# Seven half-sized products instead of eight for 40 gate-and-up pairs of a two-layer decoder

## The chip, the cores and the metric

The kernel runs on one core of a Trainium2 chip. The metric is the time of one execution on the device in microseconds (us); the kernel before takes 2120.57 us, the median of 3 runs (2119.62 to 2121.41). The core has a matrix engine (TensorE, PE in the rows; its weight loads are PEld), a vector engine (VectorE, DVE), an activation engine (ScalarE, ACT), GpSimd (POOL) and an engine that issues transfers (SyncE, SP).

## The reference

Two layers of a decoder, each a feed-forward block at half step, a token mixer and a second feed-forward block, all in float32 on 512 tokens of width 1024. What matters here is the feed-forward block:

```python
def swiglu(h, w_in, w_out):                  # h (512, 1024), w_in (1024, 2*2816), w_out (2816, 1024)
    gate, up = jnp.split(h @ w_in, 2, axis=-1)
    return (jax.nn.silu(gate) * up) @ w_out

for l in range(DEPTH):                       # DEPTH = 2
    ...                                      # mod: nine vectors from c for shifts, scales and gates
    h = modulate(rms_norm(x, norm_g[l, 0]), sh1, sc1)
    x = x + FFN_HALF * gt1[:, None, :] * swiglu(h, ffn1_in[l], ffn1_out[l])
    ...                                      # the token mixer
    h = modulate(rms_norm(x, norm_g[l, 2]), sh2, sc2)
    x = x + FFN_HALF * gt2[:, None, :] * swiglu(h, ffn2_in[l], ffn2_out[l])
return rms_norm(x, final_norm_g)
```

## The kernel before

Activations lie with channels on the 128 partitions: `hh` and `hl` hold the block's input `h` as eight chunks of 128 channels by 512 tokens. Every float32 operand of a large product is held as two parts, a high part (`whi`, `hh`, `gh`) in the matrix engine's rounded format and the rest (`wlo`, `hl`, `gl`), and a product is three matmuls, high by high, high weights by low tokens and low weights by high tokens (`mm3`, lines 414 to 420).

The 2816 hidden channels are worked in two halves of 11 *pairs*. A pair is one block of 128 gate channels and the block of 128 up channels that goes with it: two weight tiles of 128 x 1024 (eight chunks), each multiplied with all 512 tokens into a bank of PSUM, 2 x 8 x 3 = 48 matmuls of 512 columns. Then `swiglu` takes the SiLU on ACT, multiplies on DVE and splits the result into `gh` and `gl`. The first two pairs of a first half are worked together, in halves of 256 tokens, because the norm of the second half of the tokens is still being computed then. After a half's 11 pairs come its eight output blocks (each 33 matmuls).

Weights come through `Weights` (lines 138 to 187). `plan` lists them all in the order of use. `dma_to` loads one into a ring of three raw tiles (`wraw`, 512 KB each; a load of the ring waits until the tile it takes has been split), `split_to` makes `whi` on ACT and `wlo` on DVE (for the second pair of a first half, on GpSimd) in rings of four, and `use` keeps the split two tiles ahead of the products and the loads five ahead. A scheduler then sets the order on each engine: it takes the earliest work that its own model says is ready, so that queues can hold work of several pairs interleaved.

In layer 1 DVE also computes the modulation vectors beside the products (line 256, `adaw`); in layer 2 there are none left. Layer 2's first feed-forward block stands at about 1065 to 1430 us of the profile, its second at 1749 to 2108 us.

Of the kernel before, what the change touches and what calls it, by code (L numbers as in the profile page):

```python
# [139 lines left out]
class Weights:  # L140
# [5 lines left out]
        self.units, self.raw, self.hl = [], {}, {}  # L146
        self.nd = self.ns = 0

    def add(self, ap, width, pool=False):
        self.units.append((ap, width, pool))  # L150
        return len(self.units) - 1

    def dma_to(self, i):
        while self.nd < len(self.units) and self.nd <= i:
            ap, w, _ = self.units[self.nd]
            t = self.pool.tile([128, D], F32, name="wraw", tag="wraw", bufs=self.br)
            dst = t[:, :w] if len(ap.shape) == 2 else t[:, :w].rearrange("p (i n) -> p i n", n=ap.shape[2])
            self.nc.sync.dma_start(dst, ap)
            self.raw[self.nd] = t
            self.nd += 1  # L160

    def split_to(self, i):
        while self.ns < len(self.units) and self.ns <= i:
            j = self.ns
            self.dma_to(j)
            _, w, pool = self.units[j]
# [14 lines left out]
    def use(self, i):  # L181
        self.advance(i)
        return self.hl.pop(i)


class Build:
    def __init__(self, tc, a, out, dbg=None, layers=L, stop=None):
        self.tc, self.nc, self.a, self.out, self.dbg = tc, tc.nc, a, out, dbg or (lambda *k: None)
        self.layers, self.stop = layers, stop
        self.bgq = []  # L190
        self.nbank = 0
        self.sql = {}

    def bg(self, n=1):
# [233 lines left out]
    def plan(self):  # L428
        W, a = self.W, self.a
        self.u = {}  # L430
        for l in range(self.layers):
            for which in (0, 1, 2):
                if which != 1:
# [47 lines left out]
    def ffn(self, l, which):  # L481
        nc = self.nc
        w = which // 2
        gate = self.mod[l]
        gh = self.gh = self.fp.tile([128, FH, T], F32R, name="gh")
        gl = self.gl = self.fp.tile([128, FH, T], F32R, name="gl", tag="gl")
        for half in range(2):
            i = 0
            if l == 0 and which == 0 and half == 0:
# [2 lines left out]
                self.first_gl = self.last_gl  # L492
                i = FIRST
            while i < FH:
                group = [i, i + 1] if (half == 0 and i == 0) else [i]
                i += len(group)
                js = [(j, s) for j in group for s in range(2)]
# [38 lines left out]
                self.bg(self.bg_rate)  # L536
            if tail:
                self.halves(range(KC - tail, KC), out_mm, gate, 24 * which + 16)

    def swiglu(self, j, pg, pu):  # L540
        nc = self.nc
# [593 lines left out]
    def open_ffn(self, ada, first=False):  # L1135
        self.fp_cm = self.tc.tile_pool(name="ffn", bufs=1, side="right", reuse_waits="tile")
        fp = self.fp = self.fp_cm.__enter__()
        self.open_sq(fp)
        if ada:
            self.cact = fp.tile([128, D], F32, name="cact")  # L1140
            if first:
# [101 lines left out]
```

## Time and profile before

| | |
|---|---|
| median of 3 runs | 2120.57 us |
| the profiled execution's own time | 2122.84 us |
| its span in the profile | 2121.1 us |
| mean granted clock of the matrix engine | 0.996 of full |
| PE, DVE, ACT, POOL busy | 99%, 52%, 38%, 10% |
| layer 2, first feed-forward block (1064.8 to 1430) | 365.2 us; PE 363.5, DVE 132.4, ACT 111.8, POOL 15.6 busy |
| layer 2, second feed-forward block (1749 to 2108) | 359.0 us; PE 359.0, DVE 125.3, ACT 108.2, POOL 9.5 busy |

Busy times are unions: a matmul's record covers its latency, and matmuls of one stream overlap, so what one costs is the distance from one start to the next and not its duration. For DVE, ACT and POOL a duration is nearly the cost of the instruction; successive ones overlap by about 0.1 us.

### The profile page before, as it was taken

The numbers are of one execution on the slowest core, as the hardware profiler recorded it, in microseconds if no ns is written. First come the engines' busy times: TensorE is split into PE (matmuls) and PEld (weight loads), VectorE is DVE, ScalarE is ACT, GpSimd is POOL, SyncE is SP. The second block draws the span as 40 slices with busy tenths as digits, with TensorE's granted clock in tenths as the row PEclk, the third lists the DMA queues.
The fourth block names the chain that finished last, engine by engine and source line by source line (L and its number), as shares of the span: only waits on it lengthen the run. The fifth ranks groups of instructions, "written<-read, shape, count | busy, mean of one in ns | idle before, by whom it ended". The sixth has DMA issues, their size and how long they took to land.

```text
span 2121.1 us, 27803 instructions
## 1 busy us (share of the span) xinstructions
PE 2093.0 (99%) x10938; PEld 1743.2 (82%) x10938; DVE 1108.0 (52%) x1731; ACT 796.3 (38%) x1309; POOL 211.0 (10%) x196
## 2 busy tenths in 40 slices
PE   9999999999999999999999999999999999999998
PEld 7888888988965988888888888889788669888887
DVE  8894333637875799533353333335578754333332
ACT  4422323543665522222342222234527654222323
POOL 1000001312301200000110000012223020000002
PEclk9999999999999999999999999999999999999999
DMA  9894323423310699432333233235232112233322
GB/s 342 310 358 156 91 83 100 144 90 96 96 40 19 236 359 339 159 99 78 91 110 93 82 114 99 75 98 166 82 90 79 31 35 85 91 89 113 96 80 80
DMA packets 93829, 269.10 MB, mean 127 GB/s; under 512 B 10865, under 2 KB 21985, under 8 KB 93698
## 3 DMA queue, kind: packets, MB, share of 16 engines
q1 hardware_dynamic: 92018, 266.06, 38.7%
q8 instruction: 86, 1.41, 0.3%
q0 software_dynamic: 672, 0.58, 0.2%
q10 hardware_dynamic: 1008, 0.69, 0.1%
q14 instruction: 45, 0.37, 0.0%
HBM read 259.94 MB, written 2.10 MB: 124 GB/s over the span
## 4 chain that ended last, share of the span: by engine, by line
PE 96%; DVE 2%; ACT 1%; issue 1%; POOL 0%; DMA 0%; POOLq 0%; DVEq 0%; ACTq 0%
PE mm L418 26%; PE mm L419 26%; PE mm L420 26%; PE o L1062 2%; PE mm L579 1%; PE t L1052 1%; PE mm L578 1%; PE mm L580 1%; PE mm L1020 1%; PE f L419 1%; PE f L418 1%; PE f L420 1%; PE mm L1021 1%; DVE hl L349 0%; PE o L756 0%
## 5 line engine op out<-in xcount | busy, mean ns | idle before, releaser
L170 ACT ACTIVATE whi<-wraw 128x1024 fp32r<-128x1024 f32 (+3 forms) x374 | 361.1, 966 | 1054.8 <-PE mm L419 971.8
L419 PE MATMUL mm<-hl,whi 128*128 128x512 f32 (+1 forms) x1736 | 654.8, 378 | 3.1 <-DVE hl L349 3.1
L420 PE MATMUL mm<-hh,wlo 128*128 128x512 f32 (+1 forms) x1736 | 654.5, 378 | 0.0
L418 PE MATMUL mm<-hh,whi 128*128 128x512 f32 (+1 forms) x1736 | 649.3, 378 | 2.8 <-ACT hh L378 2.2
L171 DVE TENSOR_TENSOR wlo<-wraw,whi 128x1024 fp32r<-128x1024 f32 (+2 forms) x354 | 390.7, 1104 | 447.7 <-ACT whi L170 440.6
L419 PEld LDWEIGHTS mm<-hl,whi 128*128 128x128 f32 x1736 | 328.6, 189 | 62.4 <-DVE hl L349 3.7
L418 PEld LDWEIGHTS mm<-hh,whi 128*128 128x128 f32 x1736 | 326.5, 189 | 64.0 <-issue 3.1
L420 PEld LDWEIGHTS mm<-hh,wlo 128*128 128x128 f32 x1736 | 328.3, 189 | 60.5 <-issue 2.0
L419 PE MATMUL mm<-gl,whi 128*128 128x512 f32 (+1 forms) x792 | 290.2, 366 | 0.0
L420 PE MATMUL mm<-gh,wlo 128*128 128x512 f32 (+1 forms) x792 | 289.6, 366 | 0.0
L418 PE MATMUL mm<-gh,whi 128*128 128x512 f32 (+1 forms) x792 | 289.1, 365 | 0.0
L301 POOL TENSOR_TENSOR sqa<-sqa,sq 128x512 f32<-128x512 f32 (+1 forms) x44 | 51.3, 1165 | 1433.2 <-ACT sq L300 1125.8
L544 DVE TENSOR_TENSOR sg<-sg,mm 128x512 f32<-128x512 f32 x85 | 58.4, 687 | 227.5 <-PE mm L420 225.0
L256 DVE SCALAR_TENSOR_TENSOR adaw<-adaw,cact 128x1024 f32<-128x1024 f32 x144 | 171.7, 1217 | 6.6 <-ACT cact L1150 6.6
L419 PEld LDWEIGHTS mm<-gl,whi 128*128 128x128 f32 x792 | 149.4, 189 | 24.3
L420 PEld LDWEIGHTS mm<-gh,wlo 128*128 128x128 f32 x792 | 149.4, 189 | 24.0
L418 PEld LDWEIGHTS mm<-gh,whi 128*128 128x128 f32 x792 | 149.4, 189 | 24.0
L426 DVE SCALAR_TENSOR_TENSOR x<-mm,mod,x 128x512 f32<-128x512 f32 (+1 forms) x94 | 63.0, 671 | 136.5 <-PE mm L420 136.5
L1027 ACT ACTIVATE p<-mm,nm 128x128 f32<-128x128 f32 (+3 forms) x128 | 66.4, 532 | 18.9 <-DVE nm L1024 18.7
L579 PE MATMUL mm<-wlo,hh 128*128 128x256 f32 x256 | 72.9, 285 | 0.0
L578 PE MATMUL mm<-whi,hh 128*128 128x256 f32 x256 | 72.9, 285 | 0.0
L580 PE MATMUL mm<-whi,hl 128*128 128x256 f32 x256 | 72.7, 284 | 0.0
(289 smaller groups left out, 2145.2 us busy)
## 6 DMA issues: line engine op xcount, KB each, us to landing
wraw<-wfi SPq DMA_DIRECT2D x176, 512.0 KB, 3.7
adaw<-wada SPq DMA_DIRECT2D x144, 512.0 KB, 5.6
wraw<-wfo SPq DMA_DIRECT2D x64, 384.0 KB, 3.1
wraw<-wfo SPq DMA_DIRECT2D x64, 320.0 KB, 2.9
wraw<-wt SPq DMA_DIRECT2D x30, 512.0 KB, 3.7
wraw<-wn SPq DMA_DIRECT2D x16, 512.0 KB, 3.8
w<-w SPq DMA_DIRECT2D x16, 256.0 KB, 5.3
wraw<-wol SPq DMA_DIRECT2D x8, 512.0 KB, 3.7
```

Of the source, the lines that this page charges most:

```text
L170: self.nc.scalar.activation(h[:, :w], r[:, :w], AF.Copy)
L171: (self.nc.gpsimd if pool else self.nc.vector).tensor_tensor(lo[:, :w], r[:, :w], h[:, :w].bitcast(F32), op=ALU.subtract)
L256: i = nc.vector.scalar_tensor_tensor(w, w, 1.0, self.cact, op0=ALU.mult, op1=ALU.mult, accum_out=self.mod[l][:, f:f + 1])
L418: nc.tensor.matmul(out, wh[:, wk], hh[:, hk], start=start, stop=False)
L419: nc.tensor.matmul(out, wh[:, wk], hl[:, hk], start=False, stop=False)
L420: nc.tensor.matmul(out, wl[:, wk], hh[:, hk], start=False, stop=stop)
L426: nc.vector.scalar_tensor_tensor(xd, p, gate, xd, op0=ALU.mult, op1=ALU.add)
L544: nc.vector.tensor_tensor(sg, sg, pu, op=ALU.mult)
L578: nc.tensor.matmul(o, self.hh[:, k, ts], wh[:, cs], start=(k == 0 and c % 2 == 0), stop=False)
L579: nc.tensor.matmul(o, self.hh[:, k, ts], wl[:, cs], start=False, stop=False)
L580: nc.tensor.matmul(o, self.hl[:, k, ts], wh[:, cs], start=False, stop=(k == KC - 1 and c % 2 == 1))
L1027: nc.scalar.activation(p[:, h, :], s[:, i, :], AF.Exp, bias=nm[:, h:h + 1], accum_out=sm[:, h:h + 1])
```

## The change

For the 40 pairs of layer 2 that are not among the first two of a first half, the tokens are taken as two halves, A (tokens 0 to 255) and B (256 to 511), the 1024 input channels as an upper and a lower half, and the pair's gate and up weights as a 2 x 2 matrix of blocks of 512 channels by 128. The 2 x 2 by 2 x 2 block product is done with Strassen's identity in Winograd's form: seven products of half size in each dimension, each 4 chunks x 3 matmuls of 256 columns, 84 matmuls a pair.

What the seven products need beside the plain blocks are sums of blocks:

- of the weights, for each pair (`form`): a pair has four units. `a` is the gate tile as it is loaded, `s` two sums in a tile of its own (two GpSimd instructions of 512 columns, lines 189 and 190), `c` a difference written into half of the up tile (line 194), `d` a difference in half of the gate tile (line 197). All four are split, `d` at half width. The gate tile is held until `d` is split, the up tile until `c` is; a load is not issued while three raw tiles are held.
- of the tokens, once for each block (`token_forms`): three sums of 512 channels by 256 tokens, chained, each computed in two halves by DVE and GpSimd from both parts and split again, and a fourth that replaces upper channels, half B of `hh` and `hl`.

After the products, DVE and ACT put the results together in `four` (lines 635 to 647), with the SiLU, the product and the split into `gh` and `gl` as before.

```diff
@@ class Weights
-    def add(self, ap, width, pool=False):
-        self.units.append((ap, width, pool))
+    def add(self, ap, width, pool=False, form=None):
+        self.units.append((ap, width, pool, form))
...
-            ap, w, _ = self.units[self.nd]
+            ap, w, _, _ = self.units[self.nd]
+            if ap is None:
+                self.nd += 1
+                continue
+            if len(self.raw) == self.br:
+                break
...
-            r = self.raw.pop(j)
+            r = self.raw.pop(j) if form is None else self.form(j, form)
...
+    def form(self, j, form):
+        nc = self.nc
+        lo, hi = slice(0, T), slice(T, D)
+        if form == "a":
+            return self.raw[j]
+        if form == "s":
+            a, b = self.raw[j - 1], self.raw[j]
+            self.sums = s = self.sum_pool.tile([128, D], F32, name="sums", tag="cact", bufs=1)
+            nc.gpsimd.tensor_tensor(s[:, lo], b[:, lo], b[:, hi], op=ALU.add)
+            nc.gpsimd.tensor_tensor(s[:, hi], s[:, lo], a[:, lo], op=ALU.subtract)
+            return s
+        if form == "c":
+            a, b = self.raw[j - 2], self.raw.pop(j - 1)
+            nc.gpsimd.tensor_tensor(b[:, lo], a[:, lo], b[:, lo], op=ALU.subtract)
+            return b
+        a = self.raw.pop(j - 3)
+        nc.gpsimd.tensor_tensor(a[:, hi], a[:, hi], self.sums[:, hi], op=ALU.subtract)
+        return a[:, hi]
@@ plan
+                            if self.seven(l, half, i):
+                                for s, form in enumerate("ascd"):
+                                    ap = a["wfi"][l, w, half * FH + i, s] if s < 2 else None
+                                    self.u[l, w, "in", half * FH + i, form] = W.add(ap, T if form == "d" else D, form=form)
+                                continue
...
+    def seven(self, l, half, i):
+        return l > 0 and (half > 0 or i > 1)
@@ ffn
+                if self.seven(l, half, i):
+                    if self.tf is None:
+                        self.token_forms()
+                    self.seven_products(l, w, half, i)
...
+    def token_forms(self):
...
+        for name, x, y in (("1", blk(up, B), blk(up, A)), ("2", blk(dn, B), "1"), ("4", blk(dn, A), "2")):
...
+            for i, eng in enumerate((nc.vector, nc.gpsimd)):
+                ks = slice(2 * i, 2 * i + 2)
+                t = sc[:, 2 * i:2 * i + 2]
+                nc.vector.tensor_tensor(t, f(x[0][:, ks]), f(y[0][:, ks]), op=ALU.subtract)
+                eng.tensor_tensor(t, t, f(x[1][:, ks]), op=ALU.add)
+                eng.tensor_tensor(t, t, f(y[1][:, ks]), op=ALU.subtract)
+                nc.scalar.activation(th[:, ks], t, AF.Copy)
+                nc.vector.tensor_tensor(tl[:, ks], t, f(th[:, ks]), op=ALU.subtract)
+            self.tf[name] = (th, tl)
+        ds = []
+        for k in range(4):
+            t = self.sqp.tile([128, 256], F32, name="hn", tag="hn", bufs=4)
+            nc.vector.tensor_tensor(t, f(hh[:, 4 + k, B]), f(hh[:, k, B]), op=ALU.subtract)
+            nc.vector.tensor_tensor(t, t, f(hl[:, 4 + k, B]), op=ALU.add)
+            nc.vector.tensor_tensor(t, t, f(hl[:, k, B]), op=ALU.subtract)
+            ds.append(t)
+        for k in range(4):
+            nc.scalar.activation(hh[:, k, B], ds[k], AF.Copy)
+            nc.vector.tensor_tensor(hl[:, k, B], ds[k], f(hh[:, k, B]), op=ALU.subtract)
...
+    def seven_products(self, l, w, half, j):
...
+        a = use("a")
+        product(y[:, 0], a, 0, "11")
+        nc.scalar.activation(r[:, 1], y[:, 0], AF.Copy)
+        product(x[:, 0], a, T, "21")
+        s = use("s")
+        product(x[:, 1], s, T, "2")
+        nc.vector.tensor_tensor(r[:, 0:4:3], two(r[:, 1]), x, op=ALU.add)
+        product(v[:, 0], s, 0, "1")
+        c = use("c")
+        product(v[:, 1], c, 0, "3")
+        nc.vector.tensor_tensor(r[:, 1:3], two(r[:, 3]), v, op=ALU.add)
+        nc.vector.tensor_tensor(r[:, 3], r[:, 2], v[:, 0], op=ALU.add)
+        product(z[:, 0], use("d"), 0, "22")
+        product(z[:, 1], c, T, "4")
+        nc.vector.tensor_tensor(r[:, 1:3], r[:, 1:3], z, op=ALU.add)
+        nc.scalar.activation(r[:, 0:2], r[:, 0:2], AF.Silu)
+        nc.vector.tensor_tensor(sg.rearrange("p (i n) -> p i n", i=2), r[:, 0:2], r[:, 2:4], op=ALU.mult)
+        nc.scalar.activation(self.gh[:, j, :], sg, AF.Copy)
+        self.last_gl = nc.vector.tensor_tensor(self.gl[:, j, :], sg, self.gh[:, j, :].bitcast(F32), op=ALU.subtract)
```

DVE's queue in the kernel before, for two pairs of the second half of layer 2's first feed-forward block (`sg<-sg,mm` is the product with the up part, `gl` the split of a pair's result, `wlo` the splits of weights):

```order
L171 TENSOR_TENSOR wlo_10030<-wraw_9929,whi_10029 128x1024
L544 TENSOR_TENSOR sg_10022<-sg_10022,mm_9961 128x512
L171 TENSOR_TENSOR wlo_10060<-wraw_9966,whi_10059 128x1024
L546 TENSOR_TENSOR gl_8616<-sg_10022,gh_8615 128x512
L171 TENSOR_TENSOR wlo_10097<-wraw_9996,whi_10096 128x1024
L544 TENSOR_TENSOR sg_10089<-sg_10089,mm_10028 128x512
L171 TENSOR_TENSOR wlo_10127<-wraw_10033,whi_10126 128x1024
L546 TENSOR_TENSOR gl_8616<-sg_10089,gh_8615 128x512
```

The same queue in the changed kernel, for one pair, call it P, of the same half:

```order
L639 TENSOR_TENSOR four_10899<-four_10899,mm_10896 128x2x256
L643 TENSOR_TENSOR four_10899<-four_10899,mm_10897 128x512
L644 TENSOR_TENSOR four_10899<-four_10899,mm_10897 128x256
L176 TENSOR_TENSOR wlo_10985<-sums_10981,whi_10984 128x1024
L176 TENSOR_TENSOR wlo_11027<-wraw_10906,whi_11026 128x1024
L647 TENSOR_TENSOR four_10899<-four_10899,mm_10898 128x512
L176 TENSOR_TENSOR wlo_11059<-wraw_10864,whi_11058 128x512
L649 TENSOR_TENSOR sg_10900<-four_10899 128x512
L176 TENSOR_TENSOR wlo_11088<-wraw_10988,whi_11087 128x1024
L651 TENSOR_TENSOR gl_8616<-sg_10900,gh_8615 128x512
```

Four instructions a pair have become ten. The four splits (L176) are in order `s`, `c` and `d` of pair P+1 and `a` of pair P+2; the six others put pair P together.

GpSimd's queue, which holds nothing of this stretch in the kernel before (its last entries ahead of the block and the next ones at the block's end are these, in a row):

```order
L346 TENSOR_TENSOR hl_5568<-hn_8593,hh_5567 128x256
L346 TENSOR_TENSOR hl_5568<-hn_8606,hh_5567 128x256
L301 TENSOR_TENSOR sqa_10610<-sqa_10610,sq_10659 128x512
L301 TENSOR_TENSOR sqa_10610<-sqa_10610,sq_10709 128x512
L301 TENSOR_TENSOR sqa_10610<-sqa_10610,sq_10759 128x512
```

And in the changed kernel, at the start of the block (`sums` and `wraw` are the weight sums, `four` the token sums, `hl` the norm's):

```order
L370 TENSOR_TENSOR hl_5568<-hn_8606,hh_5567 128x256
L596 TENSOR_TENSOR four_8846<-four_8846,hl_5568 128x512
L597 TENSOR_TENSOR four_8846<-four_8846,t1l_8848 128x512
L197 TENSOR_TENSOR wraw_8433<-wraw_8433,sums_8635 128x512
L189 TENSOR_TENSOR sums_8993<-wraw_8918 128x512
L190 TENSOR_TENSOR sums_8993<-sums_8993,wraw_8642 128x512
L194 TENSOR_TENSOR wraw_8918<-wraw_8642,wraw_8918 128x512
L197 TENSOR_TENSOR wraw_8642<-wraw_8642,sums_8993 128x512
L596 TENSOR_TENSOR four_8846<-four_8846,hl_5568 128x512
L597 TENSOR_TENSOR four_8846<-four_8846,t2l_8860 128x512
```

After these it holds the four weight sums of each pair (L189, L190, L194, L197) and nothing else until the block's last output blocks. SP's queue keeps the same loads in the same order.

## Rows read from the trace of the kernel before

**Rows 1.** The page: busy time, and the chain that ended last.

```profile
PE 2093.0 (99%) x10938; PEld 1743.2 (82%) x10938; DVE 1108.0 (52%) x1731; ACT 796.3 (38%) x1309; POOL 211.0 (10%) x196
...
PE 96%; DVE 2%; ACT 1%; issue 1%; POOL 0%; DMA 0%; POOLq 0%; DVEq 0%; ACTq 0%
```

**Rows 2.** Timeline of PE, 512-column matmuls (start, duration); first and last of 24.

```profile
299.74 0.39 PE L420 MATMUL mm<-hh,wlo 128*128 128x512 f32 x1
...
304.95 0.39 PE L419 MATMUL mm<-hl,whi 128*128 128x512 f32 x1
```

**Rows 3.** The same for 256-column matmuls; first and last of 23.

```profile
2106.73 0.28 PE L420 MATMUL mm<-gh,wlo 128*128 128x256 f32 x1
...
2109.36 0.28 PE L418 MATMUL mm<-gh,whi 128*128 128x256 f32 x1
```

**Rows 4.** Groups by line and shape, DVE, 1070 to 1430 us (busy, mean ns).

```profile
L171 DVE TENSOR_TENSOR wlo<-wraw,whi 128x1024 fp32r<-128x1024 f32 x40 | 49.0, 1225 | 73.0 <-ACT whi L170 71.2
...
L544 DVE TENSOR_TENSOR sg<-sg,mm 128x512 f32<-128x512 f32 x22 | 15.1, 688 | 70.7 <-PE mm L420 70.0 <-ACT sg L543 0.7
L546 DVE TENSOR_TENSOR gl<-sg,gh 128x512 fp32r<-128x512 f32 x22 | 15.1, 686 | 0.0
```

**Rows 5.** The same view, ACT.

```profile
L170 ACT ACTIVATE whi<-wraw 128x1024 fp32r<-128x1024 f32 x40 | 42.4, 1061 | 140.3 <-PE mm L419 136.4 <-issue 3.9
L545 ACT ACTIVATE gh<-sg 128x512 fp32r<-128x512 f32 x22 | 13.9, 632 | 1.1 <-DVE sg L544 1.1
```

**Rows 6.** The line of the weight loads, 1070 to 1180 us: from issue to landing.

```profile
DMA to landing us min/median/max: 2.9/3.7/4.4
```

**Rows 7.** The same line, 1780 to 1880 us.

```profile
DMA to landing us min/median/max: 2.7/3.4/3.7
```

**Rows 8.** Timeline of POOL, one 512-column sum with DVE idle.

```profile
1041.63 1.29 POOL L301 TENSOR_TENSOR sqa<-sqa,sq 128x512 f32<-128x512 f32 x1 [6.20 <-ACT sq L300]
```

**Rows 9.** Timelines of POOL and of DVE, 484 to 491 us, layer 1's mixer.

```profile
485.76 2.36 POOL L171 TENSOR_TENSOR wlo<-wraw,whi 128x1024 fp32r<-128x1024 f32 x1
488.09 1.74 POOL L590 TENSOR_TENSOR sw<-sw,k_sin 128x512 f32<-128x512 f32 x1
...
485.83 2.84 DVE L592 TENSOR_TENSOR rq<-rq,sw 128x512 f32<-128x512 f32 x1 [1.18 <-POOL sw L590]
488.71 1.67 DVE L873 TENSOR_TENSOR ex<-rq,k_gq 128x512 f32<-128x512 f32 x1
```

**Rows 10.** The same two, 543 to 548 us.

```profile
544.29 3.49 POOL L590 TENSOR_TENSOR sw<-sw,k_sin 128x512 f32<-128x512 f32 x1 [4.13 <-DVE wlo L171]
...
543.07 1.21 DVE L171 TENSOR_TENSOR wlo<-wraw,whi 128x1024 fp32r<-128x1024 f32 x1
544.21 0.67 DVE L592 TENSOR_TENSOR qrot<-qrot,sw 128x512 f32<-128x512 f32 x1
544.81 0.68 DVE L591 TENSOR_TENSOR qrot<-qraw,k_cos 128x512 f32<-128x512 f32 x1
545.41 1.21 DVE L171 TENSOR_TENSOR wlo<-wraw,whi 128x1024 fp32r<-128x1024 f32 x1
```

**Rows 11.** The same two and PE at layer 2's first norm, 1063 to 1080 us.

```profile
1063.41 2.39 POOL L171 TENSOR_TENSOR wlo<-wraw,whi 128x1024 fp32r<-128x1024 f32 x1 [0.38 <-PE rb L325]
...
1063.44 1.66 DVE L342 SCALAR_TENSOR_TENSOR hn<-x,mod,rb 128x256 f32<-128x256 f32 x4 [1.01 <-PE rb L325]
...
1064.80 0.60 PE L418 MATMUL mm<-hh,whi 128*128 128x256 f32 x3
...
1068.72 0.39 PE L419 MATMUL mm<-hl,whi 128*128 128x256 f32 x1 [1.13 <-DVE hl L349]
...
1078.44 1.27 DVE L349 SCALAR_TENSOR_TENSOR hl<-hn,mod,hh 128x256 fp32r<-128x256 f32 x3
```

**Rows 12.** Stretches: span, busy time of each engine, granted clock, DMA share, GB/s.

```profile
1066.00:1070.00 4.00, 2.87 (x22) 2.67 (x22) 4.00 (x6) 1.89 (x6) 3.25 (x2) 1.00 0.64 153
...
1749.00:2108.00 359.00, 359.00 (x1719) 303.55 (x1719) 125.30 (x157) 108.17 (x148) 9.46 (x9) 1.00 0.29 88
```

More of the change, by code (lines that the diff above doesn't have):

```diff
@@ L165, in split_to @@
             self.dma_to(j)
-            _, w, pool = self.units[j]
-            r = self.raw.pop(j)
+            _, w, pool, form = self.units[j]
+            r = self.raw.pop(j) if form is None else self.form(j, form)
             h = self.pool.tile([128, D], F32R, name="whi", tag="whi", bufs=self.b)
@@ L190, in __init__ @@
         self.bgq = []
-        self.nbank = 0
+        self.nbank = self.nbank8 = 0
         self.sql = {}
@@ L484, in ffn @@
         gate = self.mod[l]
+        self.tf = None
         gh = self.gh = self.fp.tile([128, FH, T], F32R, name="gh")
@@ L494, in ffn @@
             while i < FH:
+                if self.seven(l, half, i):
+                    if self.tf is None:
+                        self.token_forms()
+                    self.seven_products(l, w, half, i)
+                    i += 1
+                    self.bg(self.bg_rate)
+                    continue
                 group = [i, i + 1] if (half == 0 and i == 0) else [i]
@@ L538, in ffn @@
                 self.halves(range(KC - tail, KC), out_mm, gate, 24 * which + 16)
+    def token_forms(self):
+        nc, fp, hh, hl = self.nc, self.fp, self.hh, self.hl
+        A, B = slice(0, 256), slice(256, 512)
+        up, dn = slice(0, 4), slice(4, 8)
+        f = lambda t: t.bitcast(F32)
+        blk = lambda ks, ts: (hh[:, ks, ts], hl[:, ks, ts])
+        self.tf = {}
+        sc = fp.tile([128, D], F32, name="four", tag="four", bufs=1).rearrange("p (i n) -> p i n", i=4)
+        for name, x, y in (("1", blk(up, B), blk(up, A)), ("2", blk(dn, B), "1"), ("4", blk(dn, A), "2")):
+            y = self.tf.get(y, y) if isinstance(y, str) else y
+            th, tl = (fp.tile([128, D], F32R, name=f"t{name}{p}", tag="adaw", bufs=6).rearrange("p (k n) -> p k n", k=4)
+                      for p in "hl")
+            for i, eng in enumerate((nc.vector, nc.gpsimd)):
[17 more added lines that the diff above has]
+            nc.vector.tensor_tensor(hl[:, k, B], ds[k], f(hh[:, k, B]), op=ALU.subtract)
+        self.tf["11"], self.tf["21"], self.tf["22"], self.tf["3"] = blk(up, A), blk(dn, A), blk(dn, B), blk(up, B)
@@ new lines, in bank8, with product, two @@
+    def bank8(self):
+        self.nbank8 += 1
+        return self.pt([128, 2, 256], ("mm", "mm", "mm", "f", "t", "t", "t", "o")[self.nbank8 % 8], name="mm")
+    def seven_products(self, l, w, half, j):
+        nc = self.nc
+        def product(out, wt, c0, form):
+            h = self.tf[form]
+            for k in range(4):
+                self.mm3(out, wt, slice(c0 + 128 * k, c0 + 128 * k + 128), (h[0][:, k], h[1][:, k]), slice(None),
+                         k == 0, k == 3)
+        def two(t):
+            return t[:, None, :].to_broadcast([128, 2, 256])
+        use = lambda form: self.use(l, w, "in", half * FH + j, form)
+        y, x, v, z = (self.bank8() for _ in range(4))
+        r = self.fp.tile([128, D], F32, name="four", tag="four", bufs=1).rearrange("p (i n) -> p i n", i=4)
+        sg = self.fp.tile([128, T], F32, name="sg", tag="sg", bufs=2)
+        a = use("a")
[17 more added lines that the diff above has]
+        self.last_gl = nc.vector.tensor_tensor(self.gl[:, j, :], sg, self.gh[:, j, :].bitcast(F32), op=ALU.subtract)
@@ L1138, in open_ffn @@
         self.open_sq(fp)
+        self.W.sum_pool = fp
         if ada:
```

## The prediction

> **What bounds the kernel now.** The page comes first: PE is busy 99% of the span, DVE 52%, ACT 38%, POOL 10%, and the chain that ended last lies 96% on PE [rows 1]. The windows of the changed stretch follow: in layer 2's second block PE is busy all of 359.0 us at a granted clock of 1.00 (the 2.4 GHz level), DVE 125.3 us, POOL 9.5 [rows 12]. So matmuls taken away are worth their full price as long as nothing else becomes late. What does become late cannot be read from busy shares; it needs the waits, and the price of two engines working at once. I therefore looked last at the places where POOL and DVE work side by side [rows 9 to 11], since the changed block is the first one where POOL works all through.
>
> **What the matmuls give.** Matmuls of 512 columns start every (304.95 - 299.74) / 23 = 0.2265 us [rows 2], those of 256 every (2109.36 - 2106.73) / 22 = 0.1195, say 0.12 us [rows 3]. A pair was 48 x 0.2265 = 10.87 us and becomes 84 x 0.12 = 10.08 us. That is 0.79 us a pair and 40 x 0.79 = **-31.7 us** for all. It is less than the eighth that goes, 1.36 us, because a matmul of 256 columns costs more than half of one of 512.
>
> The Trainium skill (TensorE: Matmul & The Clock Gate, "Back-to-back issue gap") gives a full-clock matmul of N columns N / 2.4 + 2.5 ns, that is 109 ns for 256 and 216 for 512; an estimate by that page would be 1.19 us a pair, -47 us in all. The rows here show 120 and 227 ns, and the rows decide.
>
> **What the other engines get, per pair.** DVE: 1024-column splits cost 1.225 us each with the overlap of neighbours (1.14 from start to start [rows 10]), 512-column operations 0.69 [rows 4] (0.60 from start to start [rows 10]). Three wide splits, one narrow one, the product and the split of the result, three 512-column additions out of PSUM and one of 256 columns come to about 3 x 1.225 + 6 x 0.69 + 0.42 = 8.2 us of 10.08. ACT: three wide splits at 1.06, a narrow one, `gh` at 0.63 [rows 5], SiLU and a copy, some 5.4 us. POOL: 4 x 1.29 = 5.2 us [rows 8]. Each alone would fit beside PE. They do not lie side by side, however.
>
> **POOL and DVE take turns.** In layer 1's mixer a DVE operation of 512 columns with two SBUF inputs (0.67 to 0.69 elsewhere) takes 2.84 us, because POOL began 0.07 us before it: it ends at 488.67, 0.55 us after POOL's 485.76 + 2.36; the next one takes 1.67 behind POOL's 1.74 [rows 9]. The other way round, a POOL operation that costs 1.29 alone [rows 8] takes 3.49 when four DVE operations run through from 544.21 on [rows 10]: it ends at 547.78, 1.16 us after the last of them (545.41 + 1.21). DVE operations that read one input from elsewhere are not held: four beside a POOL split of 2.39 us start 0.41 apart [rows 11]. So an SBUF-only operation of either engine costs about its full duration less some 0.14 us after the other's end, and the two sum. I take 1.16 for a POOL sum, 1.09 for a wide split and 0.60 and 0.69 for the others behind one another. The splits, and all token sums, are of this kind; the additions out of PSUM are not.
>
> The Trainium skill (SBUF — State Buffer, "Who interferes with whom") says the same of the two: the shared pair of ports is an exclusive lock, a DVE instruction with two SBUF inputs contends with a GpSimd instruction that reads, and whoever issues first holds it for the whole instruction. Rows 10 go further than that sentence, since POOL there waits through several DVE instructions.
>
> **The ring.** The new wait is this one. There are three raw tiles. A gate tile is now held until `d` is split, the last of its pair's four units, and the up tile of the next pair is loaded into it. SP waits there for DVE's narrow split (line 176), and the loads behind it in SP's queue wait too. From that split on, everything in the loop depends on what is ahead of it:
>
> - the load, issue to landing: medians 3.7 [rows 6] and 3.4 [rows 7], about 3.6;
> - POOL's two sums for `s` (lines 189, 190): 2 x 1.29 = 2.58;
> - POOL's sum for `c` (194), with the port in its hands while ACT makes `whi` of `s` (1.06, beside it): 1.29;
> - DVE's split of `s`: 1.09; POOL's `d` (197): 1.16; DVE's split of `c`: 1.09;
> - line 647 of the pair before, which stands ahead in DVE's queue: 0.60; the split of `d`: 0.69.
>
> Together 12.1 us a pair, against 10.08 on PE. PE waits at the third product (line 444, `s` by token sum 2), which needs the split of `s`; what stands behind it on PE waits too, and a pair takes 12.1. If the split of `c` gets the port before line 197 the sum is the same within 0.1. The trace before shows no such loop, so its bounds are: from below 10.9, if POOL and DVE did not hold one another up (3.6 + 2.58 + 1.06 + 1.15 + 1.15 + 0.60 + 0.69); from above 13.3, if one more wide split gets in front of POOL, as the run of DVE operations in rows 10 does. I take 12.1, since rows 9 to 11 have the same operations on the same two engines, and 2.0 us of wait a pair.
>
> Not every pair pays. A first half has nine such pairs: two are worked interleaved at its start (below), then about 0.5 us for the entry into the loop and 5 x 2.0 = 10.5 us, with the others covered by what was loaded ahead. The second half has eleven: eight output blocks of 33 matmuls stand ahead of it (60 us), so it begins with full rings and by the order three pairs run free, one waits 1.2, seven wait 2.0: 15.2 us. That is 25.7 us a block, 51.4 us for two.
>
> **The start of a block.** The token sums need the finished norm; its last operation ends at 1078.44 + 1.27 = 1079.7, 14.9 us after the group of the first two pairs began [rows 11]. From there DVE has 18 operations of 512 columns (0.60), 16 of 256 (0.40), seven splits (1.15) and six operations of the first pairs (0.60) ahead of the last token sum: 28.9 us, so 43.8 after the group's start. POOL's part of the token sums and the weight sums among them are twelve more, 12 x 1.16 = 13.9, and 57.7 if every one is in series. PE would reach the last token sum after 192 matmuls, some 1.1 us of waits as they now are (row of 1066 to 1070 [rows 12]) and 144 more: 41.4. So PE loses 2.4 to 16.3 us; the middle of the two is 9.3, a walk through the two queues gave about 10, and I take 10 a block, **20 us** for two.
>
> **Sum.** -31.7 + 51.4 + 20 = +39.7 us: the profiled execution goes from 2122.84 to about 2162.5, and the median, 2.3 us less, from 2120.57 to **about 2160 us**. The 24 pairs that wait (twelve a block) move the sum by 2.4 us for each 0.1 us of the period.
>
> **Rivals.** (1) *No turns, or a shorter load*: a period of 10.9 leaves 0.8 x 24 = 19 us of waits and some 3 for the pairs at the loop's entry, and the starts cost their lower bound, 2 x 2.4: -31.7 + 22 + 5 = -5, about 2116 us, not slower. For it: every engine has time enough on average. Against it: rows 9 to 11. It decides where line 176's splits keep 1.2 us beside POOL's sums. (2) *The loop is hidden* and only PE counts: about 2089 us. It would need the up tile to be loaded earlier than `d` is split, and three tiles do not allow that. (3) *POOL is kept waiting*: 13.3 us a period adds 24 x 1.2 = 29, about 2189 us. For it: the four DVE operations in a row of rows 10; against it: DVE's queue in the loop waits for ACT between two splits, so POOL mostly finds an opening. (4) *The clock falls* to 1.2 GHz in stretches where PE waits: a pair would take about 84 x 0.24 = 20.2 us, 8 more than the loop, and four such pairs a block add 64, about 2225 us. Against it: from 1066 to 1070 PE is busy 2.87 of 4.00 us and the granted clock is still 1.00 [rows 12]; the loop leaves PE idle 2 of 12.
>
> **Chances.** The loop at 11.5 to 12.7 us with the starts as priced: 0.74 (2135 to 2182). Rival (1) 0.09, (2) 0.03, (3) 0.10, (4) 0.04. A measurement of this kernel tells 0.2%, 4.2 us, from no change. Of rival (1) about half lies within it and the rest splits to both sides, so faster 0.07, same 0.05, slower 0.88. The range, 2120 to 2195, holds the likeliest case, most of (1) and all of the nearer part of (3).
>
> **What would show it.** Right: in later pairs of a half PE's third product begins after a wait of about 2 us released by DVE's `wlo` of `s` (line 176); pairs are 12.1 us apart, 256-column matmuls still 0.12; SP's loads wait for the narrow `wlo`; splits last over 2 us where POOL works; PE waits some 10 us in all for token sums; the clock stays 1.00. Wrong: if POOL's sums and DVE's splits overlap at full speed (then rival 1), if the loads land well under 3.4 us, if PE's wait is at another product or none, or if the clock drops. The forecast fails as a whole if the period is under 11.

## The result and the profile after

The changed kernel takes 2144.27 us (median of 4 runs, 2144.06 to 2148.38), the one before 2120.1 beside it: 1.18% slower, ratio 1.0118, 95% interval [1.0101, 1.0136], +24.2 us. Forecast were +39.7 us, about 2160 us, in a range of 2120 to 2195. The profiled execution has a span of 2146.6 us, 25.5 more than before.

The page of the changed kernel (busy time, and engines on the chain that ended last), against [rows 1]:

```profile
PE 2085.3 (97%) x12378; PEld 1801.0 (84%) x12378; DVE 1374.5 (64%) x2039; ACT 883.8 (41%) x1449; POOL 497.7 (23%) x368
...
PE 79%; DVE 9%; POOL 4%; DMA 3%; ACT 3%; issue 2%; POOLq 0%; DVEq 0%; ACTq 0%; SPq 0%
```

PE is still busy 97% of the time, and yet only 79% of the chain is PE's: between its matmuls the end is now handed through DVE, POOL, ACT and a weight load. The chain says so, the busy share doesn't. Where it happens is seen by halves. These are the products of the first and of the second half of layer 2's first block, from the first matmul to the first of the output blocks; first the kernel before, then the changed one (columns as in [rows 12]):

```profile
1064.80:1189.00 124.20, 122.48 (x634) 105.25 (x634) 50.51 (x68) 43.24 (x66) 6.51 (x6) 1.00 0.31 92
1248.80:1368.50 119.70, 119.70 (x529) 99.15 (x529) 39.62 (x43) 33.84 (x44) 0.00 (x0) 1.00 0.31 93
```

```profile
1064.90:1203.10 138.20, 125.44 (x959) 123.04 (x958) 119.72 (x155) 64.68 (x101) 77.58 (x48) 0.94 0.23 77
1263.00:1380.70 117.70, 113.30 (x926) 111.54 (x925) 95.36 (x106) 53.98 (x74) 66.19 (x40) 1.00 0.30 96
```

The first half became 14.0 us longer, the second 2.0 us *shorter*. The output blocks between them last 59.8 and 59.9 us. In the second block the second half gets 2.9 us shorter (from 119.7 to 116.8), and what lies ahead of it, from the end of the first block's output on, 16.2 longer; 1.7 of these are in the mixer, which the change leaves alone (see the first experiment). Apart from that, the whole loss lies in the first halves. The first half's granted clock of 0.94, where it was 1.00, is the first thing that the forecast had not expected.

### The ring in the second half

PE's waits in the later pairs of the second half of the changed kernel (timeline of PE; in brackets the idle time and its releaser):

```profile
1328.92 0.39 PE L444 MATMUL mm<-t2h,wlo 128*128 128x256 f32 x1 [0.76 <-DVE wlo L176]
...
1340.16 0.39 PE L444 MATMUL mm<-t2h,wlo 128*128 128x256 f32 x1 [0.75 <-DVE wlo L176]
...
1351.40 0.39 PE L444 MATMUL mm<-t2h,wlo 128*128 128x256 f32 x1 [0.76 <-DVE wlo L176]
```

The place is the one forecast: third product, low part of `s`. The period is 1351.40 - 1340.16 = 11.24 us, not 12.1 (one of the five in a row is 10.96), and six pairs of eleven wait. One turn of the loop, from the timelines of SP, POOL, ACT and DVE of the same kernel:

```profile
1342.36 12.77 SPq L163 DMA_DIRECT2D wraw<-wfi  x4
...
1345.77 1.85 POOL L189 TENSOR_TENSOR sums<-wraw 128x512 f32<-128x512 f32 x1 [4.52 <-DMA wraw<-wfi]
1347.70 1.30 POOL L190 TENSOR_TENSOR sums<-sums,wraw 128x512 f32<-128x512 f32 x1
1348.95 1.29 POOL L194 TENSOR_TENSOR wraw<-wraw 128x512 f32<-128x512 f32 x1
1350.20 2.29 POOL L197 TENSOR_TENSOR wraw<-wraw,sums 128x512 f32<-128x512 f32 x1
...
1349.03 1.06 ACT L175 ACTIVATE whi<-sums 128x1024 fp32r<-128x1024 f32 x1 [3.63 <-POOL sums L190]
...
1340.12 2.21 DVE L176 TENSOR_TENSOR wlo<-wraw,whi 128x1024 fp32r<-128x1024 f32 x1
1342.26 0.68 DVE L647 TENSOR_TENSOR four<-four,mm 128x512 f32<-128x512 f32 x1
1342.85 0.68 DVE L176 TENSOR_TENSOR wlo<-wraw,whi 128x512 fp32r<-128x512 f32 x1
...
1350.12 1.23 DVE L176 TENSOR_TENSOR wlo<-sums,whi 128x1024 fp32r<-128x1024 f32 x1 [1.80 <-ACT whi L175]
1351.36 2.21 DVE L176 TENSOR_TENSOR wlo<-wraw,whi 128x1024 fp32r<-128x1024 f32 x1
```

SP's first load of that row starts at 1342.36. The split of `c` ended at 1340.12 + 2.21 = 1342.33, the narrow split of `d` only at 1343.53. So the load that POOL's line 189 waits for takes the tile that the split of `c` frees, not the one that the split of `d` frees. From there: load 3.41, line 189 with its wait for the port 1.93, line 190 1.33, `whi` of `s` 1.09, `wlo` of `s` 1.24, and the split of `c` 2.21, of which 1.0 is POOL's line 197 taking its turn first. Sum 11.21. Line 194 runs beside ACT and costs nothing; line 647 and the split of `d` come behind the release.

### The clock in the first half

PE's three long waits at the start of the first block, and the windows behind the first two and behind a short one of the second half (columns as before; the granted clock is third from last):

```profile
1096.31 0.38 PE L444 MATMUL mm<-t1h,wlo 128*128 128x256 f32 x1 [1.89 <-DVE wlo L176]
...
1108.89 0.39 PE L442 MATMUL mm<-t2h,whi 128*128 128x256 f32 x1 [3.31 <-ACT whi L175]
...
1120.37 0.39 PE L443 MATMUL mm<-t4l,whi 128*128 128x256 f32 x1 [2.24 <-DVE t4l L599]
```

```profile
1094.00:1096.00 2.00, 0.42 (x4) 0.21 (x2) 2.00 (x2) 2.00 (x6) 1.17 (x1) 1.00 0.00 0
1096.00:1098.00 2.00, 1.70 (x9) 1.70 (x10) 2.00 (x4) 1.02 (x2) 0.00 (x0) 0.69 0.05 8
1098.00:1100.00 2.00, 2.00 (x12) 2.00 (x11) 2.00 (x5) 0.63 (x1) 0.00 (x0) 0.50 0.45 111
...
1110.00:1112.00 2.00, 2.00 (x13) 2.00 (x13) 2.00 (x3) 0.70 (x2) 2.00 (x2) 0.60 0.00 0
1112.00:1114.00 2.00, 2.00 (x12) 2.00 (x12) 2.00 (x2) 0.00 (x0) 1.92 (x2) 0.54 0.00 0
...
1364.00:1366.00 2.00, 2.00 (x19) 2.00 (x18) 1.84 (x4) 0.89 (x3) 0.00 (x0) 1.00 0.31 47
```

PE resumes, and for 3 to 4 us from then on the granted clock is 0.50, the 1.2 GHz level: 12 matmuls in a 2 us window that calls itself fully busy, where the last row has 19. Call this a dip. There are five in this half (the other two follow waits of 0.94 us just after one of 1.05, and of 1.75), and none behind the six waits of 0.62 to 0.76 us in the second half. By the mean of 0.94 they cost 138.2 x 0.06 = 8.3 us. The same sum for the first half of the second block gives 132.7 x 0.04 = 5.3 us:

```profile
1766.00:1898.70 132.70, 119.05 (x928) 115.40 (x927) 116.01 (x139) 59.35 (x89) 74.65 (x46) 0.96 0.21 71
```

The comparison with a kernel without the sums (below) comes to much the same for the first block: of the 22.0 us that the half is longer than there, 11.6 are idle time (138.2 - 125.44 against 116.2 - 115.05), and the other 10 are time in which PE was busy, but took longer. The profiled execution is no exception: over the whole span the mean granted clock is 0.988 to 0.990 in each of the four runs of the changed kernel, and 0.993 to 0.998 in the runs of the kernel before.

The kernel before has such a dip too, at the start of the second block, behind waits of 0.81 and 0.97 us; it lies inside the 359.0 us for which [rows 12] gives 1.00:

```profile
1747.89 0.39 PE L419 MATMUL mm<-hl,whi 128*128 128x256 f32 x1 [0.97 <-DVE hl L349]
...
1750.00:1752.00 2.00, 2.00 (x11) 2.00 (x11) 1.76 (x5) 1.70 (x5) 0.59 (x1) 0.50 0.26 104
```

### The profile page after: what moved, and what is told of

The parts are those of the page before. It is cut to its first block, busy times and chain, and to the rows that moved or that the text cites. A ratio compares the mean times of both kernels' runs of the same rounds, so it can differ in the third digit from the quotient of the medians.

```text
span 2146.6 us, 31570 instructions
## 1 busy us (share of the span) xinstructions
PE 2085.3 (97%) x12378; PEld 1801.0 (84%) x12378; DVE 1374.5 (64%) x2039; ACT 883.8 (41%) x1449; POOL 497.7 (23%) x368
## 4 chain that ended last, share of the span: by engine, by line
PE 79%; DVE 9%; POOL 4%; DMA 3%; ACT 3%; issue 2%; POOLq 0%; DVEq 0%; ACTq 0%; SPq 0%
PE mm L444 20%; PE mm L442 20%; PE mm L443 20%; DVE wlo L176 4%; DMA wraw<-wfi 3%; ACT whi L175 2%; POOL sums L189 2%; PE o L1175 2%; POOL sums L190 2%; PE mm L692 1%; PE t L1165 1%; PE mm L691 1%; PE mm L693 1%; PE mm L1133 1%; PE f L443 1%
## 5 line engine op out<-in xcount | busy, mean ns | idle before, releaser
L175 ACT ACTIVATE whi<-wraw 128x1024 fp32r<-128x1024 f32 (+4 forms) x414 | 384.2, 931 | 785.8 <-PE mm L443 667.1
L176 DVE TENSOR_TENSOR wlo<-wraw,whi 128x1024 fp32r<-128x1024 f32 (+4 forms) x394 | 447.6, 1140 | 286.6 <-ACT whi L175 282.5
L443 PE MATMUL mm<-hl,whi 128*128 128x512 f32 (+1 forms) x1736 | 588.4, 340 | 6.1 <-DVE hl L610 3.5
L444 PE MATMUL mm<-hh,wlo 128*128 128x512 f32 (+1 forms) x1736 | 586.6, 340 | 1.5 <-DVE wlo L176 1.4
L442 PE MATMUL mm<-hh,whi 128*128 128x512 f32 (+1 forms) x1736 | 582.4, 340 | 3.7 <-ACT hh L402 2.3
L189 POOL TENSOR_TENSOR sums<-wraw 128x512 f32<-128x512 f32 x40 | 65.9, 1648 | 286.5 <-DMA wraw<-wfi 210.1
L175 ACT ACTIVATE whi<-sums 128x1024 fp32r<-128x1024 f32 x40 | 42.4, 1060 | 111.1 <-POOL sums L190 100.3
L657 DVE TENSOR_TENSOR sg<-sg,mm 128x512 f32<-128x512 f32 x45 | 30.8, 685 | 87.3 <-PE mm L444 85.4
L197 POOL TENSOR_TENSOR wraw<-wraw,sums 128x512 f32<-128x512 f32 x40 | 84.2, 2105 | 3.6 <-issue 2.4
L176 DVE TENSOR_TENSOR wlo<-sums,whi 128x1024 fp32r<-128x1024 f32 x40 | 53.4, 1335 | 38.6 <-ACT whi L175 38.6
```

The source lines that it names most:

```text
L189: nc.gpsimd.tensor_tensor(s[:, lo], b[:, lo], b[:, hi], op=ALU.add)
L197: nc.gpsimd.tensor_tensor(a[:, hi], a[:, hi], self.sums[:, hi], op=ALU.subtract)
L442: nc.tensor.matmul(out, wh[:, wk], hh[:, hk], start=start, stop=False)
L443: nc.tensor.matmul(out, wh[:, wk], hl[:, hk], start=False, stop=False)
L444: nc.tensor.matmul(out, wl[:, wk], hh[:, hk], start=False, stop=stop)
```

## The experiments

The table gives each kernel's time (medians of 4 to 10 runs; before 2120.1 to 2120.8 beside them), its ratio to the kernel before with the interval, and in its profile the products of the two halves of layer 2's first block in us, cut as above. What each kernel is stands below. Those without a sum don't compute the reference.

| kernel | us | ratio | 1st half | 2nd half |
|---|---|---|---|---|
| before | 2120.6 | 1 | 124.2 | 119.7 |
| changed | 2144.3 | 1.0118 [1.0101, 1.0136] | 138.2 | 117.7 |
| no token, no weight sums | 2092.3 | 0.9867 [0.9853, 0.9882] | 116.2 | 110.9 |
| no weight sums | 2100.4 | 0.9907 [0.9893, 0.9922] | 123.3 | 110.8 |
| no token sums | 2110.7 | 0.9956 [0.9940, 0.9972] | 120.9 | 116.6 |
| no `d` sum | 2117.4 | 0.9981 [0.9972, 0.9991] | 130.5 | 110.9 |
| four raw tiles | 2136.2 | 1.0076 [1.0060, 1.0093] | 135.7 | 110.9 |
| wide `d` | 2148.9 | 1.0132 [1.0111, 1.0153] | 138.3 | 115.8 |
| token sums on DVE | 2145.4 | 1.0114 [1.0099, 1.0130] | 140.7 | 117.4 |
| PE filled | 2154.8 | 1.0157 [1.0133, 1.0180] | 141.0 | 118.6 |
| late, three tiles | 2113.2 | 0.9965 [0.9950, 0.9979] | 123.2 | 117.2 |
| late, four tiles | 2098.7 | 0.9896 [0.9881, 0.9910] | 119.6 | 110.9 |

**No sums at all.** Both kinds of sums taken out, `form` returning the raw tiles:

```diff
-            nc.gpsimd.tensor_tensor(s[:, lo], b[:, lo], b[:, hi], op=ALU.add)
-            nc.gpsimd.tensor_tensor(s[:, hi], s[:, lo], a[:, lo], op=ALU.subtract)
-            return s
+            return b
...
+        self.tf = {"1": blk(up, B), "2": blk(dn, B), "4": blk(dn, A)}
```

> Leaves out both the token sums and the weight sums: 84 matmuls a pair, the same splits and the same putting together. Theory (the matmuls' price is 0.12 and 0.2265 us, and nothing else of the change costs anything): 2120 - 31.7, about 2089 us, no dip of the clock in layer 2 beyond those of before. Rival (256-column streams cost more in place, or the six DVE operations a pair that put the results together hold PE up): 2098 us or more.

Between the two: 2092.3. By the halves the matmuls' price holds: 124.2 - 9 x 0.79 = 117.1 and 119.7 - 11 x 0.79 = 111.0 were to be expected, 116.2 and 110.9 came, and every inner pair of the second half is 10.08 us behind the last. Its first half:

```profile
1064.30:1180.50 116.20, 115.05 (x959) 114.85 (x959) 85.79 (x121) 61.08 (x91) 6.58 (x6) 1.00 0.30 95
```

What is missing in the total is not the change's doing. In layer 2's mixer, which all kernels have alike, PE waits 2.02 us in one place; from there to the first matmul with `ol` it takes 96.9 us here and 93.9 in the kernel before. First the kernel before, then this one, the wait and a window behind it:

```profile
1538.07 1.16 PE L817 MATMUL t<-rq,ki 64*128 64x128 f32 x16 [2.02 <-DVE ki L805]
1540.00:1542.00 2.00, 2.00 (x11) 1.60 (x10) 1.97 (x2) 0.45 (x1) 0.81 (x1) 1.00 0.65 147
...
1520.79 1.16 PE L901 MATMUL t<-rq,ki 64*128 64x128 f32 x16 [2.02 <-DVE ki L889]
1522.00:1524.00 2.00, 2.00 (x8) 1.68 (x9) 2.00 (x2) 0.60 (x1) 1.28 (x1) 0.60 0.29 66
```

Behind the same wait the clock fell in one profile and not in the other (of the twelve kernels' profiles, in eight). So the gain is there to be had, and these 116.2 and 110.9 are the measure for the others.

**One kind of sums at a time.** The token sums alone left out, and the weight sums alone, each by its part of that diff.

> Leaves out the token sums (the products that used them take plain blocks of the tokens instead). Theory (the token sums hold up the start of a block): the waits of the first pairs go, 8.0 us in the first block and 10.7 in the second, and with them dips of the clock worth 6 and 4.7 us: 29 us, about 2115 us. Rival (the weight sums on POOL hold up the starts by themselves): at most 8 us go, 2136 us or more. The period in the second halves stays 11.24 by both.

> Leaves out the four weight sums on POOL of each pair (s is split from the up tile as loaded, c and d from the raw tiles); loads, splits and tile holds stay. Theory (the loop is load 3.4, three POOL sums in it of 1.9, 1.3 and 1.1, and ACT's and DVE's splits of 1.1, 1.2 and 1.1): without the sums the loop is 3.4 + 1.06 + 1.2 + 1.1, under 7 us, so the pairs run at PE's 10.1 us; the second halves lose all their 14 us of waits and the first halves those of the later pairs, 12 to 15 with the clock, and the starts some of theirs: 2105 to 2118 us. Rival (the tile hold and the load alone bound the pairs): the period stays above 10.8, 2135 us or more.

Both theories hold in kind, and both kernels came out faster than forecast (2110.7 for about 2115, 2100.4 for 2105 at the least). Without weight sums the ring's loop is hidden (second half 110.8), without token sums it stays (116.6). In the first half each kind costs little alone, 120.9 - 116.2 = 4.7 us for the weight sums (mostly the ring's waits in the later pairs) and 123.3 - 116.2 = 7.1 for the token sums, neither with a dip of the clock. Together they cost 138.2 - 116.2 = 22.0, which is 10 more than the two add up to. By the idle times some 4 of these are further waits, and the rest is slower matmuls.

**The ring.** Three kernels, each with one change to the changed kernel: a fourth raw tile, and to make room one buffer for `sq` and `sg`; the `d` sum left out; the `d` split made as wide as the others. The main lines of the three, in this order:

```diff
+            if self.units[self.nd][3] == "s" and self.pairs % 2 == 0:
+                t = self.sum_pool.tile([128, D], F32, name="wraw", tag="extra", bufs=1)
...
-        nc.gpsimd.tensor_tensor(a[:, hi], a[:, hi], self.sums[:, hi], op=ALU.subtract)
...
-        return a[:, hi]
+        return a
```

> A fourth raw tile (taken by the up tile of every second pair; to make room, sq and sg have one buffer instead of two behind the first block). Theory (the ring closes over the tile that the split of c frees, so the load, 3.4 us, lies in the loop of 11.24 us): with a fourth tile the up tile is loaded before it is needed, the period in the second halves falls from 11.24 to PE's 10.1, and the waits of 0.9 us at the third product go: 14 us in the two second halves, 8 to 15 in the later pairs of the first halves with their dips of the clock; about 2119 us. Rival (the period is the sum of what DVE and POOL do in turns, 5 x 1.16 + 3 x 1.14 + three of 0.6, some 10 to 11 us): it stays at 10.8 or more and the time at 2135 or more.

> Leaves out one POOL sum of the four (line 197; d is split from the gate tile as loaded). It stands between DVE's splits of s and c and reads and writes nothing that c needs. Theory (DVE's split of c waits for that sum's turn at the port, 1.1 us): the split of c takes 1.2 instead of 2.2, the period in the second halves falls from 11.24 to 10.1 and the two second halves lose 10 to 13 us; with what the first halves gain 2120 to 2130 us. Rival (the sum is beside the loop, and 2.2 us has another reason): the period stays 11.24, 2144 us.

> The split of d made twice as wide (the whole gate tile is split, the lower half for nothing): ACT 0.4 and DVE 0.5 us more after the split of c. Theory (the load that the loop waits for takes the up tile, free with the split of c): the period in the second halves stays at 11.24 within 0.15, 2142 to 2150 us. Rival, as the prediction had it (the up tile of the next pair waits for the split of d): the load comes 0.5 to 0.9 us later and the period is 11.7 to 12.1; 24 pairs, 2156 us or more.

The fourth tile ends the loop: pairs 10.08 us apart, the second half 110.9, though POOL and DVE still do all their work. The rival (their turns alone fill 10 to 11 us) falls. The time of 2136 is neither side's, because the first half got only 2.5 us shorter: the starts kept their waits and dips (2.99 us at one token sum, clock 0.83 from 1100 to 1120; in the second block 0.74 and 0.83 in two windows of 20 us).

Without the `d` sum the split of `c` follows that of `s` at once. DVE's two splits with that sum (changed kernel) are above; without it, two pairs:

```profile
1325.44 1.22 DVE L176 TENSOR_TENSOR wlo<-sums,whi 128x1024 fp32r<-128x1024 f32 x1 [0.43 <-ACT whi L175]
1326.71 1.22 DVE L176 TENSOR_TENSOR wlo<-wraw,whi 128x1024 fp32r<-128x1024 f32 x1
...
1335.45 1.23 DVE L176 TENSOR_TENSOR wlo<-sums,whi 128x1024 fp32r<-128x1024 f32 x1 [0.44 <-ACT whi L175]
1336.71 1.23 DVE L176 TENSOR_TENSOR wlo<-wraw,whi 128x1024 fp32r<-128x1024 f32 x1
```

2.21 us became 1.22, two turns are 10.0 us apart, and PE no longer waits: the second half is 110.9. One POOL sum that `c` does not need was 1.0 of the 1.16 us by which the loop stood over PE's 10.08. The kernel takes 2117.4 us, a little less than the 2120 to 2130 forecast. The Trainium skill (SBUF — State Buffer, "Who interferes with whom") has it that the second engine fully blocks for the first one's whole instruction; these rows agree, with 1.0 us for a sum of 1.29.

The wide `d` tells the two tiles apart. SP's loads, POOL's first sum and DVE's splits of that kernel:

```profile
1329.91 2.06 SPq L163 DMA_DIRECT2D wraw<-wfi  x2
...
1333.20 1.37 POOL L189 TENSOR_TENSOR sums<-wraw 128x512 f32<-128x512 f32 x1 [4.40 <-DMA wraw<-wfi]
...
1327.69 2.19 DVE L176 TENSOR_TENSOR wlo<-wraw,whi 128x1024 fp32r<-128x1024 f32 x1
1330.41 1.21 DVE L176 TENSOR_TENSOR wlo<-wraw,whi 128x1024 fp32r<-128x1024 f32 x1
```

The load starts at 1329.91, 0.03 after the split of `c` (1327.69 + 2.19), though the split of `d` now ends at 1331.62. The period is 10.97 to 11.24, the second half 115.8. Had `d` freed the tile, the load would have come 1.7 us later. (The two periods, 0.27 apart, go with line 189: it takes 1.3 us where it gets the port ahead of `gl` and 1.8 where `gl` has it.)

**The start of a block.** All of the token sums on DVE:

```diff
-            for i, eng in enumerate((nc.vector, nc.gpsimd)):
+            for i, eng in enumerate((nc.vector, nc.vector)):
```

> The token sums wholly on DVE (the twelve operations of the changed kernel that GpSimd has there in two blocks go to DVE; it does 18 of 512 columns for a block's three sums and GpSimd none beside 0). Theory (what DVE and POOL do at the start stands in one series, where one costs 1.16 on POOL and 0.60 on DVE): six operations a block get 0.56 shorter each, 3 to 4 us a block, and with fewer dips of the clock 5 to 10 us in all; about 2136 us. Rival (the halves on POOL do run beside DVE): DVE's chain gets 6 x 0.6 longer a block, 2148 us or more. The second halves stay at 11.24 a pair by both.

Neither: 2145.4, as the changed kernel, the first half 140.7 at a granted clock of 0.95. Taking POOL's six operations a block out of the series gained nothing, so how much DVE and POOL have to do one after the other doesn't by itself set the price of the start. The waits only moved: the longest is now 3.23 us, for the high part of the fourth token sum. Which order of splits and sums in the queues would shorten it, this run doesn't say.

**PE kept busy.** 72 matmuls a block without use, where PE waits in pairs 2 and 3:

```diff
+        if half == 0 and j < 4:
+            for _ in range(2):
+                product(x[:, 1], a, 0, "11")
         product(x[:, 1], s, T, "2")
...
+        if half == 0 and j < 4:
+            product(z[:, 1], c, 0, "3")
         product(z[:, 1], c, T, "4")
```

> The changed kernel with 72 matmuls more a block (256 columns, their results overwritten), put where PE waits at a block's start: 24 ahead of the third product and 12 ahead of the seventh, in pairs 2 and 3 of a first half alone. Theory (the clock falls because PE stood idle there): the added matmuls take the place of the waits and no granted clock under 1.00 follows in the first 60 us; the first half of the first block, 138.2 us with 12 of waits over those of a kernel without sums and 10 of slower matmuls, comes to 116 + 8.6 of added matmuls + 3 to 7 of other waits, 128 to 132 us, less than without the added work; 2128 to 2138 us. Rival (the dips have another cause, or the waits grow by as much as PE gets ahead): the dips stay and the half takes 138 us or more, 2144 us or more.

By the figures set down for the two, the rival's side came: dips stay, the half takes 141.0 us and the whole 2154.8. A part of the theory still shows in the windows of this kernel and the wait that was left:

```profile
1096.00:1098.00 2.00, 2.00 (x19) 2.00 (x18) 2.00 (x4) 0.00 (x0) 0.00 (x0) 1.00 0.00 0
...
1114.00:1116.00 2.00, 0.06 (x1) 0.06 (x1) 2.00 (x2) 1.26 (x3) 0.70 (x1) 0.69 0.00 0
1116.00:1118.00 2.00, 2.00 (x9) 2.00 (x10) 2.00 (x4) 0.80 (x2) 0.00 (x0) 0.50 0.60 188
```

```profile
1115.94 0.58 PE L442 MATMUL mm<-t4h,whi 128*128 128x256 f32 x1 [4.49 <-ACT t4h L598]
```

The two waits of 1.89 and 3.31 us at the third and fourth products are gone, and the clock stayed at 1.00 there: the changed kernel had two dips up to 1114, this one none. Then PE waited 4.49 us in one place for the fourth token sum, where it had been 2.24, although 12 of the added matmuls stand ahead of that sum's product, and the clock fell behind it, this time for nearly 7 us. In the first half two dips are left of five (mean clock 0.96 for 0.94); but the added work is 8.6 us and the waits got only some 2 shorter, so as a remedy it fails. That the clock follows PE's idle time is supported by where the dips are and are not; which waits lower it is not shown, since the 2.02 us of the mixer did so in some profiles only. The price of the dips by themselves was not parted from the waits by any run.

**Both causes taken away.** Pairs 2 and 3 of a first half plain again (36 pairs by seven products), the token sums spread over that time on DVE; with three raw tiles, and with four ("late" in the table):

```diff
-        return l > 0 and (half > 0 or i > 1)
+        return l > 0 and (half > 0 or i > 3)
...
+                if self.tf is not None and half == 0 and 2 <= i <= 4:
+                    self.token_forms(i - 2)
```

> As the last kernel (pairs 2 and 3 of a first half plain, the token sums beside them on DVE), but with three raw tiles and all other buffers as in the changed kernel: it parts the gain of the start from that of the ring. Theory (the two are separate): the second halves are back at 117 us with 10.97 to 11.24 a pair, the first halves lose their waits for token sums and their dips of the clock but keep 0.9 to 1.2 a pair of the ring: 2099 + 2 x 6.5 + 2 x 3 to 5, about 2118 us, just under the kernel before. Rival (the fourth tile made the difference at the start too): first halves above 130 us and 2130 us or more.

> Pairs 2 and 3 of a first half are worked plainly again (36 of 44 pairs by seven products), the token sums are made beside them, one sum ahead of each of pairs 2, 3 and 4 and wholly on DVE; a fourth raw tile as before. Theory (the change loses its gain at the start of a block and in the ring, and with both covered only the matmuls count): second halves 110.9 us instead of 119.7, first halves 124.2 - 7 x 0.79 = 118.7, no dip of the clock there: 2121 - 2 x 14.3, about 2093 us. Rival (the token sums hold up the plain pairs as much as the others): 2105 us or more.

The halves of the version with four tiles:

```profile
1066.20:1185.80 119.60, 117.27 (x887) 112.81 (x887) 114.31 (x149) 62.07 (x95) 55.02 (x33) 1.00 0.29 92
1245.60:1356.50 110.90, 110.90 (x926) 110.87 (x925) 97.62 (x109) 56.79 (x75) 63.42 (x37) 1.00 0.33 103
```

It takes 2098.7 us, 1.04% less than the kernel before and the fastest that computes the reference. The clock is 1.00 in both halves, PE never stops in the second. With three tiles the starts are as good (no dip) and the ring's waits are back (117.2): 2113.2, for about 2118 forecast, so the late start is worth 31 us against the changed kernel and the fourth tile 14.5 more. The fourth tile alone, without the late start, was worth 8: it saved 2.5 us in the first block's first half and nothing in the second's, where the waits and dips of the start stayed. Forecast for both together were 2093; the first half missed by 0.9 us, its products begin at 1066.2, 1.4 us later than before, and ahead of the second block's second half 3.1 us went where 5.5 were forecast; why was not tried.

## Why the prediction was right or wrong

The sign held, the two places of the loss did, and so did the turns of POOL and DVE. The size was 1.6 times too large, +39.7 for +24.2, and that it came so near is in part luck. The period of 11.24 us lies outside the likeliest case (11.5 to 12.7), and the clock, which was to stay at 1.00, gave back a good part of what the waits fell short: the dips cost some 14 us of the two blocks by the mean clocks, and without them the rise would have been nearer 10 us than 25.

- **The matmuls, -31.7.** Right: 0.12 us each in place, 10.08 a pair, and the halves without sums came out at -8.0 and -8.8 a block, for -7.1 and -8.7.
- **POOL and DVE take turns.** Right, shown by the `d` sum. The priced durations were near: 1.0 for a turn of POOL put at 1.16, 1.24 for a split put at 1.09. One reading was off: in [rows 10] POOL's operation begins at 544.29, when the first of the four DVE operations has ended (543.07 + 1.21), so it waited through three.
- **The ring, 12.1 a pair: the step that failed.** The prediction let the up tile of the next pair go "into" the held gate tile, so that the loop closed over the split of `d`. It goes into the up tile, free with the split of `c`. That takes line 647 and the split of `d` out, 1.29 us, and the load was 3.41 for 3.6; line 194 lies beside ACT's `whi` (1.29 becomes 1.09); line 189 waits for `gl` (0.64 more), and the split of `s` takes 0.15 more. 12.1 becomes 11.2 (measured 11.24), and the excess over PE 1.16 instead of 2.0, on six pairs of a second half instead of seven and a bit. So 15.2 us became 117.7 - 110.9 = 6.8, and the second halves turned from +6.5 to -2.0 and -2.9: 8.5 and 9.4 us, which is more than the whole error of 14.2 us of the profiled span. The prediction's own sign of failure, a period under 11, came close: one period of five was 10.96.
- **The first half, +13.4 a block.** Measured +14.0 in the first block and some +14.5 in the second (16.2 less the mixer's 1.7). The agreement is luck: only half is for the reasons given. Waits were to be 20.5 (10 at the start, 10.5 in the ring); they are 11.6 over the kernel without sums, of the long ones 7.4 at the start and 3.7 in the ring. Most of the other 10 us are the clock.
- **The clock stays 1.00.** Wrong in the first halves. Rows 12 showed a stretch with 28% idle at 1.00, but its idle time is one wait of 1.13 us [rows 11]; the new waits of 1.75 to 3.31 us in one piece in that half were followed by the lower level. The argument from the share of idle time was the mistake. The trace before already had a dip, which the 1.00 of [rows 12] rounds away. The rival that had the clock fall put it in the ring of the later pairs, where it fell at most twice in a first half and not in the second half, at 64 us for what was some 14.
- **Bounds for the start, 2.4 to 16.3.** The waits fell inside; the thought behind the middle (more or less in series) did not stand, since moving POOL's share to DVE changed nothing.
- **Rival (1), 10.9 a pair.** (Its terms add up to 10.83.) Near the measured 10.96 to 11.24 in number, but for another reason: turns are taken, and two pieces less are in the loop.

## What to carry to other kernels

Trace a ring's loop by the tile that the next load really takes, and see in the order which release it waits for; the two pieces that the forecast had too many were 1.3 us a pair here. Sums that fit every engine's share of time still cost what they add to the chain from release to release, and a fourth buffer took the loop out of PE's way with all its work left in place (8 us here, 14.5 with the start mended). Don't start new serial work where PE has just caught up with its producers: two pairs of delay with the sums spread over them, which give up 0.8 us a pair, gave back 31 us.

## What was not expected of the hardware

- The granted clock fell to 0.50 for 3 to 4 us at a time behind waits of PE of 1.75 to 3.3 us (and of 0.94 after 1.05), not behind repeated single waits of 0.62 to 0.76 us, one each 11.24 us. The length of a wait alone doesn't tell: in the second block of the same profile one of 1.71 us (up to 1818.29) was followed by no dip, and the mixer's 2.02 us were followed by one in eight profiles of twelve.
- POOL, waiting at the port behind one DVE split, got it ahead of DVE's next one (line 197 in every pair of the second half), while in [rows 10] it waited through three DVE operations.
